# Down projection of a hybrid decoder layer: loads in program order, reloads spread over two loops, two more staging buffers

## The chip, the cores and the metric

The kernel runs on one core of a Trainium2 chip. The metric is the device time of one execution in microseconds, and a smaller one is better. The profile shows the core's engines: PE (TensorE, matmuls; PEld its weight loads), DVE (VectorE), ACT (ScalarE), POOL (GpSimd) and SP (SyncE). In this kernel every DMA is issued from SP, in the order in which SP's instructions stand, and SP waits at an instruction whose semaphores have not come yet.

## The reference, cut to what matters

One decoder layer for 512 tokens and a width of 1024, in float32: two attention mixers, a gated convolutional MLP and a gated embedding. The change is in the MLP's last product (the down projection) and in what is loaded beside it:

```
h  = rmsnorm(x, mlp_pre_norm)
u  = causal_dwconv(h @ w_up)                    # 1024 -> 2 * 2816
ff = (gelu(u_gate) * u_val) @ w_down            # 2816 -> 1024, the down projection
x  = x + rmsnorm(ff, mlp_post_norm)
e  = p @ w_ple
x  = x + sigmoid(rmsnorm(x, ple_norm) @ w_ple_gate) * e
```

## The kernel before, in words

Every float32 product is done as three matmuls: an operand is split into a high part (ACT, L72) and a low part (DVE, L73), and high x high, high x low and low x high are added in PSUM (`mm3`).

**Up projection.** A loop over 22 pairs of 128 columns. PE writes `pu`; ACT and DVE do the convolution and the gelu (L816 to L824). After every second pair, `ff_sums` (L786 to L799) makes from the product `X` of one *chunk* c (0 to 10, 256 hidden units each) the sums that the down projection needs, splits them, keeps the first four in SBUF (`FF[c]`, in the tiles with the tags xh/xl for chunks 0 to 3, kT/qT for 4 to 7, fA/fB for 8 to 10) and writes the others to DRAM: `d1[c]` (512 KB, from `f2h` and `X`) and `d2[c]` (256 KB). The last chunk is chunk 10. `X` and `f2h` live in a pool `qp` that closes when the up projection ends.

**Down projection.** It is a fast product in the manner of Strassen and Winograd, so that seven products do the work of eight. It has three loops over the 11 chunks:

- Loop 1 (L874 to L890): two loads of `w_down` into `raw` tiles per chunk, here called **r1(c)** (L877, 512 KB) and **r2(c)** (L878, 256 KB). DVE forms differences of them (L882 needs r1; L883 and L884 need r2 too) in `T13`/`T2`; ACT and DVE split them; PE does 24 matmuls per chunk, for the products M1, M5, M7 and M6. M1 needs r1 alone; M5 and M7 share one split of 128x1024 that needs r2 as well.
- Loop 2 (L922 to L934): one load per chunk, **raw(c)** (L924, 512 KB), and the reloaded `d1[c]`, **p1(c)** (L915, 512 KB). PE does 12 matmuls per chunk (M1 goes on, and M3).
- Loop 3 (L947 to L952): the product M4, six matmuls per chunk, from the reloaded `d2[c]`, **p2(c)** (L945, 256 KB), and the differences `T4[c]` that loop 2 made.

p1(0..3) goes into the tile with the tag xh, p1(4..7) into xl, and p1(8..10) into xh again: p1(8) can be loaded only once PE has done with p1(0..3). After the loops come the norms (`post_norm`, L725 to L735), transposes (`to_hT`) and the products `pg` and `pe` of the embedding. The norms need the residual `xn` (four reloads of 512 KB, L894) and two gain vectors (L656, 512 KB each).

**What sets the order.** The program is written as a sequence, and a scheduler puts each engine's instructions in an order of its own before the kernel is built; on the chip each engine then keeps that order. Loads into `raw` tiles take a ring of three buffers: a load waits until DVE and ACT have read the buffer's last contents. `hi` and `lo` tiles have rings of four. A pool that is opened where a closed one lay waits for the last readers of what lay there.

Of the kernel before, what the change touches and what calls it, by code (L numbers as in the profile page):

```python
# [8 lines left out]
F32 = mybir.dt.float32  # L9
F32R = mybir.dt.float32r  # L10
# [5 lines left out]
P = 128  # L16
S = 512
NB = 4
# [19 lines left out]
def hybrid_kernel(ctx, tc, T):  # L38
    nc = tc.nc
    act, dve, pool = nc.scalar, nc.vector, nc.gpsimd  # L40
    order = mybir.DependencyInfo(mybir.DependencyClass.NoSync, mybir.DependencyReason.DATA)
# [21 lines left out]
    def opened(**kw):  # L63
        cm = tc.tile_pool(reuse_waits="tile", **kw)
        p = cm.__enter__()
        return p, lambda: cm.__exit__(None, None, None)

    def f32(ap):
        return ap.bitcast(F32)

    def split(hi, lo, src):
        act.activation(hi, src, AF.Copy)  # L72
        dve.tensor_tensor(lo, src, f32(hi), ALU.subtract)  # L73

    def mm3(out, lh, ll, rh, rl, start, stop):
        pe.matmul(out, lh, rh, start=start, stop=False)
        pe.matmul(out, lh, rl, start=False, stop=False)
        pe.matmul(out, ll, rh, start=False, stop=stop)

    def hot(f, *args):  # L80
        with tc.high_priority(HOT):
            return f(*args)
# [23 lines left out]
    xp, close_xp = opened(name="xp", bufs=1, side="left")  # L106
# [14 lines left out]
    W = {"rings": RA, "raw": 0, "hi": 0, "lo": 0}  # L121

    def wtile(kind, dt):
        ring = W["rings"][kind]
        n = W[kind] % sum(c for _, c in ring)
        W[kind] += 1
        for p, c in ring:
            if n < c:
                return p.tile([P, 1024], dt, name="w" + kind, tag="w" + kind, bufs=c)
            n -= c  # L130
# [31 lines left out]
    xh = xp.tile([P, 8, S], F32R, name="xh", tag="xh")  # L162
    xl = xp.tile([P, 8, S], F32R, name="xl", tag="xl")
# [487 lines left out]
    mxl = xp.tile([P, 8, S], F32R, name="mxl", tag="xl")  # L651
    p3 = [accT, accT, scT, scT, scT, ptT, ptT, pvT]

    def loadgain(src):
        t = res["bcp"].tile([P, D], F32, name="gain", tag="gain", bufs=2)
        nc.sync.dma_start(t, src.partition_broadcast(P))  # L656
        return t

    for m in range(8):
# [13 lines left out]
    for f in (close_ca, close_wk, close_gap, close_sp, close_cqp, close_kvp, close_yp):  # L673
# [4 lines left out]
             raw=0, hi=0, lo=0)  # L678
    ck, close_ck = opened(name="ck", bufs=1, side="right")
    fp, close_fp = opened(name="fp", bufs=1, side="right")  # L680

    res = {}

    def open_res():
        b, close_b = opened(name="bcp", bufs=1, side="right")
        x, close_x = opened(name="xnp", bufs=1, side="right")
        res.update(bcp=b, xn=x.tile([P, NB, D], F32, name="xn"), close=(close_x, close_b))

    def close_res():
        for f in res["close"]:  # L690
            f()
# [12 lines left out]
    def banks(n, name):  # L704
        return [bank(n, name) for _ in range(2)]
# [14 lines left out]
    def post_norm(n, ps, gp, gn):  # L720
        xn = res["xn"]
        t = ck.tile([P, D], F32, name="t", tag="t", bufs=3)
        s1, s2, r1, r2, v = (small(f"q{i}", 2 if i == 0 else 1) for i in range(5))
        for h in range(2):
            act.activation(t[:, h * S:(h + 1) * S], ps[h], AF.Square, accum_out=s1[:, h:h + 1])  # L725
        dve.tensor_scalar(v, s1[:, 0:1], 1.0 / D, EPS, ALU.mult, ALU.add)
        dve.scalar_tensor_tensor(v, s1[:, 1:2], 1.0 / D, v, ALU.mult, ALU.add)  # L727
        pool.tensor_tensor(r1, v, mhalf[:, :1], ALU.pow)  # L728
        for h in range(2):
            w = slice(h * S, (h + 1) * S)  # L730
            dve.scalar_tensor_tensor(t[:, w], ps[h], r1, gp[:, w], ALU.mult, ALU.mult)
        dve.tensor_tensor(xn[:, n, :], t, xn[:, n, :], ALU.add)
        act.activation(t, xn[:, n, :], AF.Square, accum_out=s2)
        rsqrt(r2, s2, 1.0 / D, 1)
        dve.scalar_tensor_tensor(t, xn[:, n, :], r2, gn, ALU.mult, ALU.mult)  # L735
        return t
# [17 lines left out]
    for n in range(NB):  # L754
        nc.sync.dma_start(res["xn"][:, n, :], T["x"][n * P:(n + 1) * P, :])
    xd = [dp.tile([P, D], F32, name=f"xd{n}", tag=f"xd{n}") for n in range(NB)]
    g_post, g_next = loadgain(T["attn_post"]), loadgain(T["mlp_pre"])
    ts = {}
    for blocks in ((0, 1), (2,), (3,)):
# [11 lines left out]
    NC = NPAIR // 2  # L771
# [3 lines left out]
    d1 = [dp.tile([P, 2, 2, 256], F32, name=f"d1_{c}", tag=f"d1_{c}") for c in range(NC)]  # L775
    d2 = [dp.tile([P, 2, 256], F32, name=f"d2_{c}", tag=f"d2_{c}") for c in range(NC)]
# [80 lines left out]


    close_qp()
    open_res()  # L860
    xn = res["xn"]
    vp, close_vp = opened(name="vp", bufs=1, side="right")
    T2t = [hp.tile([P, 8, S], F32, name=f"T2{i}", tag=f"hT{i}") for i in range(2)]
    T2 = [T2t[c // 8][:, c % 8] for c in range(NC)]
    T13 = [T2t[1][:, 4 + 2 * i:6 + 2 * i].rearrange("p a t -> p (a t)") for i in range(2)]
    B1, B2 = slice(0, S), slice(S, 2 * S)
# [3 lines left out]
    def mms(ps, lhs, rhs, start, stop):  # L870
        for b in range(2):
            t = slice(b * P, (b + 1) * P)
            mm3(ps[b], lhs[0][:, t], lhs[1][:, t], *rhs, start, stop)

    for c in range(NC):
        r1, r2 = wtile("raw", F32), wtile("raw", F32)
        nc.sync.dma_start(r1, T["wd"][2 * c])  # L877
        nc.sync.dma_start(r2[:, :S], T["wd"][2 * c + 1][:, B2])  # L878
        t13 = T13[c % 2]
        h1, l1, h2, l2 = (wtile(k, F32R) for k in ("hi", "lo", "hi", "lo"))  # L880
        split(h1[:, B1], l1[:, B1], r1[:, B1])
        dve.tensor_tensor(t13[:, B1], r1[:, B2], r1[:, B1], ALU.subtract)  # L882
        dve.tensor_tensor(t13[:, B2], r2[:, :S], r1[:, B2], ALU.subtract)  # L883
        dve.tensor_tensor(T2[c], r2[:, :S], t13[:, B1], ALU.subtract)  # L884
        split(h2, l2, t13)
        split(h1[:, B2], l1[:, B2], T2[c])
        rhs = {"M1": (h1[:, B1], l1[:, B1]), "M5": (h2[:, B1], l2[:, B1]),
               "M7": (h2[:, B2], l2[:, B2]), "M6": (h1[:, B2], l1[:, B2])}
        for m, s in zip(order4, (0, 1, 3, 2)):
            mms(M[m], [t[:, s] for t in FF[c]], rhs[m], c == 0, c == NC - 1)  # L890

    g_post, g_next = loadgain(T["mlp_post"]), loadgain(T["ple_norm"])
    for n in range(NB):
        nc.sync.dma_start(xn[:, n, :], xd[n])  # L894
    T4k = qkp.tile([P, 8, S], F32, name="T4k", tag="kT")
    T4q = qkp.tile([P, 8, S], F32, name="T4q", tag="qT")
    T4 = [T4k[:, c] for c in range(8)] + [T4q[:, 0], T4q[:, 1], vp.tile([P, S], F32, name="T4v")]
    U, V12, C22 = ([T4q[:, 2 + 2 * i + b] for b in range(2)] for i in range(3))

    def drain():  # L900
# [6 lines left out]
            dve.tensor_tensor(C22[b], M["M5"][b], U[b], ALU.add)  # L907

    hot(drain)
    p1 = []  # L910
    for c in range(NC):
        if c % 4 == 0:
            t = xp.tile([P, 4, 2, 2, 256], F32R, name="p1", tag="xl" if c == 4 else "xh")
        p1.append(t[:, c % 4])
        nc.sync.dma_start(f32(p1[c]), d1[c])  # L915
    M3 = banks(3, "M3")

    def m3(c, rhs):
        mms(M3, [p1[c][:, i, 1] for i in range(2)], rhs, c == 0, c == NC - 1)

    late = None
    for c in range(NC):  # L922
        raw = wtile("raw", F32)
        nc.sync.dma_start(raw, T["wd"][2 * c + 1])  # L924
        h, l = wtile("hi", F32R), wtile("lo", F32R)
        split(h, l, raw)
        dve.tensor_tensor(T4[c], raw[:, B1], T2[c], ALU.subtract)
        for b in range(2):
            t = slice(b * P, (b + 1) * P)
            lh, ll = p1[c][:, 0, 0, t], p1[c][:, 1, 0, t]  # L930
            for x, y in ((lh, h), (lh, l), (ll, h)):
                pe.matmul(M["M1"][b], x, y[:, B1], start=False, stop=c == NC - 1 and x is ll, skip_group_check=True)
        if late:
            m3(*late)  # L934
        late = (c, (h[:, B2], l[:, B2]))
# [3 lines left out]
    for n in range(2):  # L939
        dve.tensor_tensor(V12[n], M3[n], V12[n], ALU.add)  # L940
        ts[n] = post_norm(n, (M["M1"][n], V12[n]), g_post, g_next)
    p2t = [fp.tile([P, 6, 2, 256], F32R, name="p2", tag=t) for t in ("fA", "fB")]
    p2 = [p2t[c // 6][:, c % 6] for c in range(NC)]
    for c in range(NC):
        nc.sync.dma_start(f32(p2[c]), d2[c])  # L945
    M4 = banks(2, "M4")
    for c in range(NC):  # L947
        if c % 2 == 0:
            h, l = wtile("hi", F32R), wtile("lo", F32R)
        w = slice(c % 2 * S, (c % 2 + 1) * S)  # L950
        split(h[:, w], l[:, w], T4[c])
        mms(M4, [p2[c][:, i] for i in range(2)], (h[:, w], l[:, w]), c == 0, c == NC - 1)  # L952
# [59 lines left out]
    raw = wtile("raw", F32)  # L1012
    nc.sync.dma_start(raw, T["pT"].rearrange("p a b -> p (a b)"))
    split(ph.rearrange("p a b -> p (a b)"), pl.rearrange("p a b -> p (a b)"), raw)
    for k in range(2):
        raw = wtile("raw", F32)
# [12 lines left out]
    for n in (2, 3):  # L1029
        for half in range(2):  # L1030
# [4 lines left out]
            gate_mms(g, (n,), (half,))  # L1035
            finish(n, half, g[n, half])

    close_vp()
    close_res()
    for f in (close_fp, close_ck, close_rawb, close_qkp, close_rawp, close_psp,  # L1040
              close_hp, close_wb, close_wa, close_xp, close_cpool, close_dp):
        f()
# [89 lines left out]
```

## Time and profile before

| | |
|---|---|
| median of 3 runs (lowest to highest) | 756.83 us (754.61 to 758.09) |
| the profiled execution: its time, its span | 756.0 us, 754.2 us |
| PE busy | 730.6 us (97%) |
| DVE, ACT busy | 533.3 us (71%), 362.8 us (48%) |
| DMA moved | 99.90 MB, mean 132 GB/s |
| chain that ended last | PE 77%, DVE 11%, DMA 9% |

The span runs from the first to the last instruction; the profiled execution's time is 1.8 us longer. On the time line, the up projection ends at 564.8 us, loop 1 runs to 640.1 us, loops 2 and 3 to 687.2 us, and the rest of the kernel takes the last 67 us. A row of the timeline begins with its start and its length in us; the bracket at its end is the idle time before it and what ended it. "Landing" is the time from the issue of a DMA on SP until its data are there.

### The profile page before, as it was taken

The page shows a single profiled execution, that of the slowest core. Times are in us where ns is not written, and L with a number is a line of the kernel's source. Part 1 is how long each engine was busy: PE and PEld are TensorE (multiplying, and loading weights), DVE is VectorE, ACT ScalarE, POOL GpSimd, SP SyncE. Part 2 cuts the span into 40 slices and gives each one's busy share as a digit, 9 for nine tenths or more (in the row PEclk, how much of TensorE's full clock was granted, in tenths as well). Part 3 has the DMA queues.
Part 4 walks back from the last instruction along what each step waited for, and adds up shares of the span by engine and source line. Part 5 has one row for each costly group of instructions (what it writes and reads, how often), then busy time and mean ns, then how long its engine had stood idle before and what let it go on. Part 6 is the DMA issues. An engine that isn't in the chain of part 4 may idle for free.

```text
span 754.2 us, 9531 instructions
## 1 busy us (share of the span) xinstructions
PE 730.6 (97%) x3496; PEld 606.4 (80%) x3496; DVE 533.3 (71%) x939; ACT 362.8 (48%) x634; POOL 49.8 (7%) x46
## 2 busy tenths in 40 slices
PE   9999999999999989999999999999999869998997
PEld 8988878778888868898888888888887658876886
DVE  6568787986785493848776777676759657789832
ACT  5843677755453243627435444544435234266631
POOL 0104023000000070200000000000000000001000
PEclk9999999999999999999999999999999979999999
DMA  8612221121122455324343434334314874943311
GB/s 301 243 42 63 60 84 43 57 79 63 56 84 59 164 189 174 129 95 140 126 152 127 152 128 139 130 105 143 116 66 157 319 294 151 378 151 112 113 56 56
DMA packets 36239, 99.90 MB, mean 132 GB/s; under 512 B 4481, under 2 KB 8577, under 8 KB 36193
## 3 DMA queue, kind: packets, MB, share of 16 engines
q1 hardware_dynamic: 36192, 99.30, 38.8%
q8 instruction: 27, 0.44, 0.3%
q14 instruction: 20, 0.16, 0.1%
HBM read 85.98 MB, written 12.85 MB: 131 GB/s over the span
## 4 chain that ended last, share of the span: by engine, by line
PE 77%; DVE 11%; DMA 9%; issue 2%; ACT 1%; SPq 0%; ACTq 0%; DVEq 0%
PE pu L56 29%; PE psg L56 11%; DMA wraw<-in_wd 7%; PE yo L56 6%; PE pg L56 6%; DVE wlo L73 3%; PE puh L56 3%; PE M L56 3%; PE psA L56 3%; PE psba L56 3%; PE psC L56 2%; PE psB L56 2%; PE pe L56 1%; PE scm L56 1%; PE pb L56 1%
## 5 line engine op out<-in xcount | busy, mean ns | idle before, releaser
L56 PE MATMUL pu<-hT,whi 128*128 128x512 f32 x640 | 197.0, 389 | 0.0
L72 ACT ACTIVATE whi<-wraw 128x1024 fp32r<-128x1024 f32 (+4 forms) x109 | 106.5, 979 | 162.9 <-PE pu L56 75.2
L73 DVE TENSOR_TENSOR wlo<-wraw,whi 128x1024 fp32r<-128x1024 f32 (+2 forms) x103 | 119.4, 1161 | 65.7 <-ACT whi L72 62.0
L56 PEld LDWEIGHTS pu<-hT,whi 128*128 128x128 f32 x640 | 120.1, 188 | 25.0
L56 PE MATMUL pu<-hT,wlo 128*128 128x512 f32 x320 | 124.5, 389 | 0.0
L56 PEld LDWEIGHTS pu<-hT,wlo 128*128 128x128 f32 x320 | 60.1, 188 | 12.3
L56 PE MATMUL psg<-xh,whi 128*128 128x512 f32 x128 | 51.7, 404 | 1.0 <-DVE ga L422 0.9
L56 PE MATMUL psg<-xl,whi 128*128 128x512 f32 x128 | 51.3, 401 | 0.0
L56 PE MATMUL psg<-xh,wlo 128*128 128x512 f32 x128 | 51.2, 400 | 0.0
L56 PE MATMUL M<-whi,p 128*128 128x512 f32 x132 | 41.4, 393 | 1.0 <-ACT whi L72 1.0
L72 ACT ACTIVATE whi<-T 128x1024 fp32r<-128x1024 f32 (+1 forms) x22 | 17.8, 838 | 38.3 <-DVE T L883 38.2
L816 ACT ACTIVATE cv<-pu,pp 128x512 f32<-128x512 f32 x40 | 30.6, 765 | 9.1 <-PE pu L56 9.1
L817 DVE SCALAR_TENSOR_TENSOR cv<-pu,pp,cv 128x511 f32<-128x511 f32 x40 | 29.8, 745 | 4.3 <-ACT cv L816 4.3
L818 DVE SCALAR_TENSOR_TENSOR cv<-pu,pp,cv 128x510 f32<-128x510 f32 x40 | 29.9, 747 | 1.1
L819 ACT ACTIVATE cv<-cv 128x512 f32<-128x512 f32 x22 | 13.9, 632 | 34.2 <-DVE cv L818 34.2
L56 PEld LDWEIGHTS M<-whi,p 128*128 128x128 f32 x132 | 24.7, 188 | 6.8 <-ACT whi L72 1.4
L728 POOL TENSOR_TENSOR q<-q,mhalf 128x1 f32<-128x1 f32 x8 | 5.3, 674 | 375.5 <-DVE q L727 369.7
L56 PEld LDWEIGHTS psg<-xh,whi 128*128 128x128 f32 x128 | 24.5, 191 | 6.5 <-DVE ga L422 1.1
L56 PEld LDWEIGHTS psg<-xl,whi 128*128 128x128 f32 x128 | 24.4, 191 | 5.0 <-issue 0.2
L56 PEld LDWEIGHTS psg<-xh,wlo 128*128 128x128 f32 x128 | 24.4, 190 | 4.9
L56 PE MATMUL M<-wlo,p 128*128 128x512 f32 x66 | 26.0, 394 | 0.1
L670 POOL TENSOR_TENSOR gx<-gx,ga 128x512 f32<-128x512 f32 x8 | 14.8, 1869 | 133.3 <-DVE gx L669 133.3
(304 smaller groups left out, 1585.9 us busy)
## 6 DMA issues: line engine op xcount, KB each, us to landing
wraw<-in_wup SPq DMA_DIRECT2D x44, 512.0 KB, 3.5
wraw<-in_wd SPq DMA_DIRECT2D x22, 512.0 KB, 4.3
wraw<-in_wg SPq DMA_DIRECT2D x16, 512.0 KB, 3.3
p<-d SPq DMA_DIRECT2D x11, 512.0 KB, 9.6
wraw<-in_wo SPq DMA_DIRECT2D x8, 512.0 KB, 4.1
wraw<-in_wpg SPq DMA_DIRECT2D x8, 512.0 KB, 3.4
d<-f2h SPq DMA_DIRECT2D x11, 256.0 KB, 3.1
d<-X SPq DMA_DIRECT2D x11, 256.0 KB, 2.0
```

The source lines that it names most:

```text
L56: pe.chain(out, nc.tensor.matmul(out, *a, **k))
L72: act.activation(hi, src, AF.Copy)
L73: dve.tensor_tensor(lo, src, f32(hi), ALU.subtract)
L670: pool.tensor_tensor(ta, ta, ga[:, m, :], ALU.add)
L728: pool.tensor_tensor(r1, v, mhalf[:, :1], ALU.pow)
L816: act.activation(c, u, AF.Identity, scale=w2, bias=cb)
L817: dve.scalar_tensor_tensor(c[:, 1:], u[:, :S - 1], w1, c[:, 1:], ALU.mult, ALU.add)
L818: dve.scalar_tensor_tensor(c[:, 2:], u[:, :S - 2], w0, c[:, 2:], ALU.mult, ALU.add)
L819: act.activation(cs[0], cs[0], AF.Gelu_apprx_tanh)
```

## The change

All loads of the down projection go through a helper `load`, which ties each load to the one before it, so that SP issues them in the order of the program. The reloads p1(0) to p1(7) stand in loop 1, behind the chunks 5 to 10; p1(8) to p1(10), the gains, the residual and p2 stand in loop 2. For loop 1 the ring of raw buffers has two more (pool `rx`, five in all), which lie where the closed pool `qp` lay; the pools of the gains and the residual are opened after loop 1, where they were opened before it.

```diff
-    def loadgain(src):
+    def loadgain(src, go=nc.sync.dma_start):
         t = res["bcp"].tile([P, D], F32, name="gain", tag="gain", bufs=2)
-        nc.sync.dma_start(t, src.partition_broadcast(P))
+        go(t, src.partition_broadcast(P))
         return t
...
     close_qp()
-    open_res()
-    xn = res["xn"]
     vp, close_vp = opened(name="vp", bufs=1, side="right")
+    T4v = vp.tile([P, S], F32, name="T4v")
+    rx, close_rx = opened(name="rx", bufs=1, side="right")
+    R2 = W["rings"]["raw"]
+    W["rings"]["raw"] = R2 + [(rx, 2)]
+    loads = []
+
+    def load(dst, src):
+
+        i = nc.sync.dma_start(dst, src).ins
+        if loads:
+            tc.add_manual_dep(i, loads[-1], order, reason="load order")
+        loads.append(i.name)
+
+    p1 = []
+
+    def load_p1(c):
+        if c % 4 == 0:
+            load_p1.t = xp.tile([P, 4, 2, 2, 256], F32R, name="p1", tag="xl" if c == 4 else "xh")
+        p1.append(load_p1.t[:, c % 4])
+        load(f32(p1[c]), d1[c])
...
     for c in range(NC):
         r1, r2 = wtile("raw", F32), wtile("raw", F32)
-        nc.sync.dma_start(r1, T["wd"][2 * c])
-        nc.sync.dma_start(r2[:, :S], T["wd"][2 * c + 1][:, B2])
+        load(r1, T["wd"][2 * c])
+        load(r2[:, :S], T["wd"][2 * c + 1][:, B2])
...
-    g_post, g_next = loadgain(T["mlp_post"]), loadgain(T["ple_norm"])
-    for n in range(NB):
-        nc.sync.dma_start(xn[:, n, :], xd[n])
+        for i in {5: (0,), 6: (1,), 7: (2,), 8: (3,), 9: (4, 5), 10: (6, 7)}.get(c, ()):
+            load_p1(i)
+
+    close_rx()
+    W["rings"]["raw"] = R2
+    open_res()
+    xn = res["xn"]
...
-    p1 = []
-    for c in range(NC):
-        if c % 4 == 0:
-            t = xp.tile([P, 4, 2, 2, 256], F32R, name="p1", tag="xl" if c == 4 else "xh")
-        p1.append(t[:, c % 4])
-        nc.sync.dma_start(f32(p1[c]), d1[c])
...
     for c in range(NC):
         raw = wtile("raw", F32)
-        nc.sync.dma_start(raw, T["wd"][2 * c + 1])
+        load(raw, T["wd"][2 * c + 1])
+        if c in (4, 5, 6):
+            load_p1(c + 4)
+        if c in (3, 4, 5, 6):
+            load(xn[:, c - 3, :], xd[c - 3])
+        if c == 2:
+            g_post, g_next = loadgain(T["mlp_post"], load), loadgain(T["ple_norm"], load)
+        if c == 7:
+            p2t = [fp.tile([P, 6, 2, 256], F32R, name="p2", tag=t) for t in ("fA", "fB")]
+            p2 = [p2t[c // 6][:, c % 6] for c in range(NC)]
+        if c >= 7:
+            for i in range(3 * (c - 7), min(3 * (c - 6), NC)):
+                load(f32(p2[i]), d2[i])
...
-    p2t = [fp.tile([P, 6, 2, 256], F32R, name="p2", tag=t) for t in ("fA", "fB")]
-    p2 = [p2t[c // 6][:, c % 6] for c in range(NC)]
-    for c in range(NC):
-        nc.sync.dma_start(f32(p2[c]), d2[c])
```

**SP at the end of the up projection, before.** `wraw` with in_wd is a load of w_down (128x1024 is r1, 128x512 is r2; here r1(0), r2(0), r1(1), then r2(1) and so on); d1_9, d2_9, d1_10 and d2_10 are the writes of the last two chunks to DRAM.

```order
L877 DMA wraw_5012<-in_wd 128x1024
L878 DMA wraw_5013<-in_wd 128x512
L877 DMA wraw_5053<-in_wd 128x1024
L798 DMA d1_9_3118<-f2h_4828 128x512
L799 DMA d2_9_3129<-f2h_4828 128x256
L798 DMA d1_9_3118<-X_4749 128x512
L799 DMA d2_9_3129<-X_4749 128x256
L878 DMA wraw_5054<-in_wd 128x512
L877 DMA wraw_5094<-in_wd 128x1024
```

The first chunk's two loads and one of the second stand ahead of the writes of chunk 9; those of chunk 10 come ten rows further down. The same place with the change:

```order
L869 DMA wraw_5009<-in_wd 128x1024
L798 DMA d1_9_3118<-f2h_4828 128x512
L799 DMA d2_9_3129<-f2h_4828 128x256
L798 DMA d1_9_3118<-X_4749 128x512
L799 DMA d2_9_3129<-X_4749 128x256
L798 DMA d1_10_3119<-f2h_4984 128x512
L799 DMA d2_10_3130<-f2h_4984 128x256
L798 DMA d1_10_3119<-X_4905 128x512
L799 DMA d2_10_3130<-X_4905 128x256
L869 DMA wraw_5010<-in_wd 128x512
L869 DMA wraw_5050<-in_wd 128x1024
L869 DMA wraw_5051<-in_wd 128x512
```

r1(0) alone is still ahead; r2(0) (`wraw_5010`) and every load behind it now stand behind the writes of chunk 10.

**DVE at the same place, with the change.** L901 to L903 are what L882 to L884 were (the differences of a chunk of w_down); L817 to L796 finish chunk 10 of the up projection.

```order
L901 TENSOR_TENSOR T_5000<-wraw 128x512
L817 SCALAR_TENSOR_TENSOR cv<-pu,pp,cv 128x511
L818 SCALAR_TENSOR_TENSOR cv<-pu,pp,cv 128x510
L824 TENSOR_TENSOR X<-cv 128x2x256
L788 TENSOR_TENSOR X<-X 128x256
L790 TENSOR_TENSOR X<-X 128x256
L791 TENSOR_TENSOR X<-X 128x256
L73 TENSOR_TENSOR fffB<-X,fffA 128x1024
L796 TENSOR_TENSOR X<-X,f2h 128x768
L902 TENSOR_TENSOR T_5000<-wraw 128x512
L903 TENSOR_TENSOR T_4999<-wraw,T_5000 128x512
```

Before, the rows of chunk 10 stood between those of the down projection's chunks 0 to 3; now they stand in one piece, between the first difference of chunk 0 and its second.

**SP in loop 2, with the change.** From raw(4) (`wraw_5567`) to raw(7) (`wraw_5631`); the bracket names the engines that a load waits for (DMAHW is an earlier DMA).

```order
L869 DMA wraw_5567<-in_wd 128x1024 [waits DMAHW6_49,DMAHW4_49,DVE_49]
L869 DMA p1_5569<-d1_8_3117 128x1024 [waits PE_49]
L869 DMA xn_5477<-xd1_2797 128x1024
L869 DMA wraw_5589<-in_wd 128x1024 [waits DMAHW7_49,DVE_49]
L869 DMA p1_5569<-d1_9_3118 128x1024 [waits DMAHW0_49]
L869 DMA xn_5477<-xd2_2798 128x1024 [waits DMAHW1_49]
L869 DMA wraw_5610<-in_wd 128x1024 [waits DMAHW2_49,DVE_49]
L869 DMA p1_5569<-d1_10_3119 128x1024 [waits DMAHW3_49]
L869 DMA xn_5477<-xd3_2799 128x1024 [waits DMAHW4_49]
L869 DMA wraw_5631<-in_wd 128x1024 [waits DMAHW5_49,DVE_49]
```

And before, where p1(8) to p1(10) stood behind raw(7), and three loads of w_down behind them:

```order
L924 DMA wraw_5608<-in_wd 128x1024
L945 DMA p2_5752<-d2_9_3129 128x512
L945 DMA p2_5752<-d2_10_3130 128x512
L924 DMA wraw_5627<-in_wd 128x1024
L915 DMA p1_5494<-d1_8_3117 128x1024
L915 DMA p1_5494<-d1_9_3118 128x1024
L915 DMA p1_5494<-d1_10_3119 128x1024
L924 DMA wraw_5646<-in_wd 128x1024
L924 DMA wraw_5665<-in_wd 128x1024
L924 DMA wraw_5684<-in_wd 128x1024
```

p1(8), which waits for PE, stood behind raw(7) (`wraw_5627`) and now stands ahead of raw(5) (`wraw_5589`); the reloads of the residual, which were issued in loop 1, now stand between the loads of w_down.

## Rows read from the trace of the kernel before

**Rows 1.** The page: PE's granted clock and the DMA engines' share in 40 slices.

```profile
PEclk9999999999999999999999999999999979999999
DMA  8612221121122455324343434334314874943311
```

**Rows 2.** Timeline of PE, the waits of the down projection and the stages' first matmuls.

```profile
567.24 1.89 PE L56 MATMUL M<-whi,ffxh 128*128 128x512 f32 x7 [0.89 <-ACT whi L72]
...
606.61 3.78 PE L56 MATMUL M<-whi,ffkT 128*128 128x512 f32 x8 [5.40 <-ACT whi L72]
...
617.39 2.35 PE L56 MATMUL M<-whi,ffkT 128*128 128x512 f32 x6 [2.82 <-ACT whi L72]
...
640.11 0.62 PE L56 MATMUL M<-whi,p 128*128 128x512 f32 x2
...
663.06 1.19 PE L56 MATMUL M<-whi,p 128*128 128x512 f32 x4 [1.03 <-ACT whi L72]
...
687.19 1.03 PE L60 MATMUL ptr<-ident,t 128*128 128x128 f32 x8
```

**Rows 3.** Timeline of DVE: the difference that the second wait hung on.

```profile
604.69 0.69 DVE L883 TENSOR_TENSOR T<-wraw 128x512 f32<-128x512 f32 x1 [7.85 <-DMA wraw<-in_wd]
```

**Rows 4.** Timeline of SP, the queue ahead of that load, DMAs as issued.

```profile
588.36 0.40 SPq L878 DMA_DIRECT2D wraw<-in_wd  x1
...
591.08 2.31 SPq L894 DMA_DIRECT2D xn<-xd  x4
593.80 0.33 SPq L878 DMA_DIRECT2D wraw<-in_wd  x1
```

**Rows 5.** DMA issues, loads issued at 593.80, 566.12 and 545.39: KB, us to landing.

```profile
wraw<-in_wd SPq DMA_DIRECT2D x1, 256.0 KB, 10.9
...
wraw<-in_wd SPq DMA_DIRECT2D x1, 256.0 KB, 2.8
...
wraw<-in_wd SPq DMA_DIRECT2D x1, 512.0 KB, 3.4
```

**Rows 6.** Windows: stretch, its length, each engine's busy us, PEclk, DMA share, GB/s.

```profile
606.60:610.20 3.60, 3.59 (x9) 2.82 (x10) 2.47 (x4) 0.99 (x2) 0.00 (x0) 0.50 1.03 409
610.20:611.40 1.20, 1.20 (x5) 0.97 (x4) 0.00 (x0) 0.00 (x0) 0.00 (x0) 0.56 1.03 413
617.40:620.40 3.00, 3.00 (x9) 2.33 (x9) 2.70 (x5) 0.99 (x2) 0.00 (x0) 0.61 0.73 257
...
642.00:650.00 8.00, 8.00 (x37) 6.64 (x36) 7.18 (x11) 2.12 (x2) 0.00 (x0) 1.00 0.99 358
...
655.00:661.00 6.00, 6.00 (x29) 4.95 (x28) 2.86 (x3) 1.06 (x1) 0.00 (x0) 1.00 1.02 410
```

**Rows 7.** Timelines of ACT and DVE: one of each step that finishes an up chunk.

```profile
565.03 0.78 ACT L816 ACTIVATE cv<-pu,pp 128x512 f32<-128x512 f32 x1 [2.37 <-PE pu L56]
579.79 1.06 ACT L72 ACTIVATE fffA<-X 128x1024 fp32r<-128x1024 f32 x1
...
560.40 0.75 DVE L817 SCALAR_TENSOR_TENSOR cv<-pu,pp,cv 128x511 f32<-128x511 f32 x1 [2.72 <-ACT cv L816]
577.26 0.41 DVE L788 TENSOR_TENSOR X<-X 128x256 f32<-128x256 f32 x1
583.02 1.21 DVE L73 TENSOR_TENSOR fffB<-X,fffA 128x1024 fp32r<-128x1024 f32 x1
586.50 0.94 DVE L796 TENSOR_TENSOR X<-X,f2h 128x768 fp32r<-128x768 f32 x1
```

**Rows 8.** Groups of PE instructions from 640 to 663: count, busy us, mean ns.

```profile
L56 PE MATMUL M<-whi,p 128*128 128x512 f32 x64 | 19.9, 389 | 0.0
L56 PE MATMUL M<-wlo,p 128*128 128x512 f32 x32 | 12.4, 389 | 0.0
```

**Rows 9.** Timeline of DVE: the last difference of loop 2, and the first transposed block.

```profile
665.92 0.68 DVE L927 TENSOR_TENSOR T4v<-wraw,T 128x512 f32<-128x512 f32 x1
691.65 1.28 DVE L748 TENSOR_TENSOR h3T<-ptr,h3T 128x512 fp32r<-128x512 f32 x2
```

More of the change, by code (lines that the diff above doesn't have):

```diff
@@ L890, in hybrid_kernel @@
             mms(M[m], [t[:, s] for t in FF[c]], rhs[m], c == 0, c == NC - 1)
-    g_post, g_next = loadgain(T["mlp_post"]), loadgain(T["ple_norm"])
-    for n in range(NB):
-        nc.sync.dma_start(xn[:, n, :], xd[n])
+        for i in {5: (0,), 6: (1,), 7: (2,), 8: (3,), 9: (4, 5), 10: (6, 7)}.get(c, ()):
[4 more added lines that the diff above has]
+    xn = res["xn"]
     T4k = qkp.tile([P, 8, S], F32, name="T4k", tag="kT")
     T4q = qkp.tile([P, 8, S], F32, name="T4q", tag="qT")
-    T4 = [T4k[:, c] for c in range(8)] + [T4q[:, 0], T4q[:, 1], vp.tile([P, S], F32, name="T4v")]
+    T4 = [T4k[:, c] for c in range(8)] + [T4q[:, 0], T4q[:, 1], T4v]
     U, V12, C22 = ([T4q[:, 2 + 2 * i + b] for b in range(2)] for i in range(3))
@@ L1036, in hybrid_kernel @@
             finish(n, half, g[n, half])
+    close_res()
     close_vp()
-    close_res()
     for f in (close_fp, close_ck, close_rawb, close_qkp, close_rawp, close_psp,
```

## Prediction, made before the changed kernel was run

> **What bounds the kernel now.** I read the page's slices first [rows 1]: PE's clock and the DMA share are even everywhere but in slices 32 to 36 of 40 (585 to 680 us), where the DMA share is 0.8, 0.7, 0.4, 0.9 and 0.4 and the clock of one slice falls to 0.7. That is the down projection. The timeline of PE shows there where the time goes [rows 2]: four pauses, 0.89, 5.40, 2.82 and 1.03 us, each ended by an ACT split of freshly loaded weights. Elsewhere PE runs without a gap, so PE bounds the kernel but for these 10.1 us, and what each leaves behind: after the second and third, PE ran at 0.50, 0.56 and 0.61 of its clock, that is partly at 1.2 GHz where it had 2.4 before the pause [rows 6].
>
> The view of DVE says why the longest came: it sat 7.85 us until r2 of a chunk landed [rows 3]. That load was issued at 593.80 and took 10.9 us [rows 4, 5], against 2.8 for one of the same 256 KB on a quiet queue [rows 5]. Right ahead of it stood the four reloads of the residual, 2 MB [rows 4], which only the norms behind loop 2 read. So reloads that nothing needs yet go in front of the weights that PE needs at once. The change aims at this burst. The place to ask is therefore which load PE waits for in the new order of SP.
>
> **The change part by part.**
>
> *Burst removed from loop 1.* Residual and gains leave it, and the p1 come one or two per chunk behind a chunk's own weights. Gone are the pauses of 5.40 and 2.82 us [rows 2] and their slow clock: 3.60 us at 0.50 cost 1.8, 1.20 at 0.56 cost 0.5, 3.00 at 0.61 cost 1.2 [rows 6], and I take 0.5 more behind the last by the pattern of the first. Sum: 5.40 + 2.82 + 1.8 + 0.5 + 1.2 + 0.5 = **-12.2**. Nothing takes their place inside loop 1: a chunk brings 0.77 MB and at most two p1 (1.05 MB) in the 5.5 us or so that its 24 matmuls take, some 330 GB/s against the 410 that the queue has moved [rows 6], and five buffers hold two and a half chunks. p1(0) waits on SP until PE has done chunk 3, but by then chunks 4 and 5 are loaded. If that cover is thinner than I think, up to 2 us come back.
>
> *A new hole at the start of loop 1.* The two new buffers lie where `qp` lay, and on SP r2(0) now stands behind the four writes of chunk 10, which wait for ACT and DVE to finish that chunk. Before, r2(0) and r1(1) stood ahead even of the writes of chunk 9, and PE's seventh matmul of loop 1 began at 567.24 [rows 2]. Now PE has only M1's six matmuls of chunk 0. The chain for the seventh, from the last `pu` result: ACT L816 begins at 565.03 and takes 0.78; DVE L817, L818 and L824, three of 0.75 or less; L788, L790, L791, 0.41 each; the split on ACT 1.06 and on DVE 1.21; L796 0.94 [rows 7]: 565.03 + 0.78 + 2.25 + 1.23 + 1.06 + 1.21 + 0.94 = 572.5. From the end of such an L796 (586.50 + 0.94) over two writes to the next load (588.36) took 0.92 [rows 4, 7], so r2(0) is issued at 573.4 and lands 2.8 later [rows 5], at 576.2. From landing to PE it took 604.69 to 606.61, 1.92 [rows 2, 3]: PE goes on at 578.1, **+10.9** against 567.24. The pause of some 12 us is longer than the 5.40 that cost 2.3 of clock, so **+2.3** more. Bounds: neighbouring rows overlap by up to 0.4 in all, and the load may take the 3.4 of a 512 KB one; 12.8 to 13.8 for both. Loop 1 then ends at about +1.0, at 641.
>
> *Blocked loads in loop 2.* p1(8) goes into the tile of p1(0..3) and so waits for PE to finish chunk 3 of loop 2; the loads keep their order, so xn1, raw(5) and all behind queue up after it. Before, the three p1 of this tile stood behind raw(7), with three loads still to come, and the pause at 663.06 was 1.03 [rows 2]. With S for the start of loop 2 (640.11 before): 96 matmuls took 663.06 - 1.03 - 640.11 = 21.9 us [rows 2, 8], 0.228 each. Four chunks are 48 matmuls, so p1(8) is issued at S + 10.9. A 512 KB load alone lands in 3.4 [rows 5], and each further 512 KB takes 1.28 at 410 GB/s [rows 6]; raw(5) is the third, landing at S + 16.9, and its split is 1.06 by a row of the same shape [rows 7]: PE starts chunk 5 at S + 18.0, where chunk 4 ended at S + 13.7. From there the queue is one unbroken stream of 16.5 x 512 KB up to raw(10) (xn2, xn3, p1(9), p1(10) and nine p2 stand between the weights): S + 10.9 + 3.4 + 15.5 x 1.28 = S + 34.1. Of this the nine p2 (4.5 x 512 KB) are the small kind, and where these were queued the rate was 358 GB/s, 1.46 for 512 KB (from 642 to 650) [rows 6]; with 4.5 x 0.18 = 0.8 more, raw(10) lands at S + 34.9 and is split at S + 36.0. Then chunk 10 and M4, 78 matmuls. Loops 2 and 3 took 687.19 - 640.11 = 47.1 for 198 matmuls, less 1.03 and some 0.4 taken for slow clock behind it 0.231 each, so M4 ends at S + 36.0 + 18.0 = S + 54.0: **+6.9** against 47.1. The lower bound is raw(5)'s wait alone, 4.3 and some 1.2 of clock less the 1.4 that goes: +4.1. The upper one has the whole stream at that 358: 15.5 x 0.18 = 2.8 on top of 6.1, +8.9.
>
> The Trainium skill ("DMA: Bandwidth & Descriptors", section "Where 436 GB/s comes from") says that for transfers between HBM and SBUF the HBM side binds at about 358 GB/s. The 8 us with p2 in the queue agree with it, but the 6 us behind them do not, at 410 on this one core [rows 6], and the measurement decides; by the page the whole stream would go at that rate, and the sum would be 2.0 longer.
>
> *Residual, gains and p2 later.* Nothing waits for them: the gains land by S + 5 and the residual by S + 25, while the norms that read them come after chunk 10; the last p2 lands some 1.5 behind raw(10), and M4 comes to it ten chunks later.
>
> *The tail.* DVE is nearly full behind loop 2. From the last difference (665.92) to the first transposed block (691.65) it had 25.7 us of work [rows 9]; that block was 4.5 behind M4's end. With raw(10) landing at S + 34.9 and the same list, it comes at S + 60.6, 6.6 behind M4's end; some of the list waited for PE or POOL and shrinks. I take **+0.5** (0 to 2.1).
>
> Sum against the profiled execution's own time: 756.0 - 12.2 + 10.9 + 2.3 + 6.9 + 0.5 = **764.4**. That execution is 0.8 under the median of 756.83, inside the runs' spread. What a measurement can tell from no change is about 0.5%, 3.8 us.
>
> **The rivals.**
>
> *Faster.* The burst is the whole story, and the two new buffers fill the loop. "Perfetto Trace Analysis" in the Trainium skill (section "Identifying the Most-Contended Engine") says that the same gap coming again can mean too little SBUF for the next tile, and that would speak for five buffers. As a mechanism here: r2(0) is in SBUF when the up projection ends, and raw(5) was issued before p1(8) blocks. Then 756.0 - 12.2 - 1.4 = 742.4; with the hole of loop 2 alone, 756.0 - 12.2 + 7.4 = 751.2. For it: the two big pauses did hang on that burst. Against it: the order of SP leaves no way round the writes of chunk 10.
>
> *No change.* The hole at the start comes, but loop 2 runs as before: 756.0 + 1.0 - 1.4 = 755.6. That needs raw(5) to land some 4 us earlier than I find, hence SP to pass p1(8) by S + 7, when PE is in the middle of chunk 2. Against it: p1(8) is tied to PE.
>
> *Slower still.* The stream of loop 2 goes at 358 GB/s from raw(5) on, not only where p2 stand in it, and DVE's list ends the full 2.1 later: 756.0 + 1.0 + 8.9 + 2.1 = 768.0. For it: no row shows weights, p1, residual and p2 mixed as they will be. Against it: the stretch at 410 carried weights and p1 side by side, by the order of SP.
>
> *That the change does nothing* can be left out: SP's order has changed.
>
> **How the numbers follow.** Forecast 0.58 (its own range 760 to 767.5), slower still 0.18, no change 0.12, faster 0.12. The range of 755 to 770 takes in the no-change case, the forecast and most of the slower one, and leaves out the faster one and the far end: 0.17. Faster than -0.5% (under 753) 0.12; within 0.5% 0.13, the no-change case and a sliver of the forecast; slower (over 760.6) 0.75.
>
> **What would show it.** A pause of 10 to 12 us on PE right after six M matmuls at 566, ended by a split whose r2 was issued behind the writes from `X`; no pause above 1 us from there to the end of loop 1, which ends at 641 give or take 2; in loop 2 a pause of 4 to 5 us before chunk 5, with p1(8) issued when chunk 3 ends, and pauses below 1 us behind it; M4's end near 695. I am wrong if r2(0) is issued before 570, if raw(5) lands before PE has done chunk 4, or if loop 1 has a new pause that I took as covered.

## The result: slower by 1.35%, about as forecast

| | before | after |
|---|---|---|
| median of the compared runs, us | 757.46 (754.61 to 758.93, 4 runs) | 767.14 (766.63 to 768.39, 4 runs) |
| profiled execution, us (its span) | 756.0 (754.2) | 768.39 (766.6) |
| first matmul of loop 1 to first of loop 2 | 75.28 | 75.80 |
| first of loop 2 to first transpose | 47.08 | 55.93 |
| first transpose to the end of the span | 67.0 | 68.8 |

The ratio is 1.0135, with a 95% interval of 1.0101 to 1.0168. The forecast was 764.4 (755 to 770), with 0.75 on slower. The two spans differ by 12.4 us, the medians by 9.7, because the profiled execution of after is the slowest of its four and that of before lies 1.5 under its median. The 12.4 fall into four parts, from first matmuls: 1.24 ahead of loop 1, which begins at 566.07 where it began at 564.83 (the second kernel below differs from after in loop 2 alone and begins it at 563.78, so this is scatter), 0.52 in loop 1, 8.85 in loops 2 and 3, 1.8 in the tail.

The page's slices of after, PE's granted clock and the DMA share, show the move at once, beside those of before [rows 1]. From slice 31 on the DMA share is now even, 0.7, 0.5, 0.6, 0.6, 0.8, 0.6, where it went 0.4, 0.8, 0.7, 0.4, 0.9, 0.4. The low clock has left slice 33, the middle of loop 1, for slices 30 and 31, its start, and 35, loop 2.

```profile
PEclk9999999999999999999999999999987999899999
DMA  8711221212112633515433434343117566863311
```

The timeline of PE (start, duration, line, operation, count, idle time ahead and what ended it), in answer to [rows 2]:

```profile
566.07 0.39 PE L56 MATMUL M<-whi,ffxh 128*128 128x512 f32 x1
...
580.29 2.07 PE L56 MATMUL M<-whi,ffxh 128*128 128x512 f32 x4 [12.70 <-ACT whi L72]
...
641.87 0.63 PE L56 MATMUL M<-whi,p 128*128 128x512 f32 x2
...
661.40 2.08 PE L56 MATMUL M<-whi,p 128*128 128x512 f32 x4 [5.72 <-ACT whi L72]
...
697.80 1.09 PE L60 MATMUL ptr<-ident,t 128*128 128x128 f32 x8 [0.29 <-DVE t L735]
699.80 0.50 PE L56 MATMUL pg<-whi,h3T 128*128 128x512 f32 x1 [0.91 <-ACT h3T L747]
703.19 1.00 PE L60 MATMUL ptr<-ident,t 128*128 128x128 f32 x4 [2.19 <-DVE h3T L748]
```

The four pauses of the three loops, 10.1 us, have become two of 18.4: one at the seventh matmul of loop 1, one before chunk 5 of loop 2. Between 580 and 641 PE does not stop. The queue of SP, in answer to [rows 4], has the cause of both:

```profile
573.88 0.42 SPq L799 DMA_DIRECT2D d<-X  x1
574.40 16.25 SPq L869 DMA_DIRECT2D wraw<-in_wd  x11
...
642.28 0.37 SPq L869 DMA_DIRECT2D wraw<-in_wd  x1
652.99 0.33 SPq L869 DMA_DIRECT2D p<-d  x1
653.36 0.43 SPq L869 DMA_DIRECT2D xn<-xd  x1
653.89 0.38 SPq L869 DMA_DIRECT2D wraw<-in_wd  x1
```

r2(0) goes out at 574.40, right behind the writes from `X` of chunk 10. In loop 2, SP issues nothing between raw(4) at 642.28 and p1(8) at 652.99, 10.7 us later; that p1 waits for PE, and raw(5) stands two loads behind it, although its buffer was free: the last reader of raw(2), which had lain there, was DVE's split at 642.06, 1.21 long.

The timeline of DVE has the finish of chunk 10 (L796), the landing of r2(0) and the first transposed block (compare [rows 3, 9]):

```profile
572.53 0.95 DVE L796 TENSOR_TENSOR X<-X,f2h 128x768 fp32r<-128x768 f32 x1
578.46 0.69 DVE L902 TENSOR_TENSOR T<-wraw 128x512 f32<-128x512 f32 x1 [4.98 <-DMA wraw<-in_wd]
...
677.83 0.69 DVE L955 TENSOR_TENSOR T4v<-wraw,T 128x512 f32<-128x512 f32 x1 [0.91 <-DMA wraw<-in_wd]
...
702.45 1.27 DVE L748 TENSOR_TENSOR h3T<-ptr,h3T 128x512 fp32r<-128x512 f32 x2
```

Windows of after (length, busy time of PE, PEld, DVE, ACT, POOL, then granted clock, DMA share, GB/s), in answer to [rows 6]:

```profile
578.00:582.00 4.00, 1.71 (x4) 1.42 (x5) 3.53 (x5) 2.10 (x3) 0.00 (x0) 0.50 0.99 338
...
660.00:666.00 6.00, 4.60 (x11) 3.69 (x12) 3.40 (x4) 2.11 (x2) 0.00 (x0) 0.52 1.02 416
666.00:672.00 6.00, 5.95 (x25) 4.33 (x25) 3.05 (x4) 1.78 (x2) 0.00 (x0) 1.00 1.04 396
672.00:678.00 6.00, 5.88 (x23) 3.67 (x22) 3.31 (x4) 1.50 (x3) 0.00 (x0) 1.00 1.04 397
```

After each pause PE comes back at 0.50 of its clock, 1.2 GHz, for some 4 us. And the stream of loop 2, with weights, p1, residual and p2 in it, ran at 396 to 416 GB/s from 660 on; in its first 6 us, from 654, it had moved 330.

### The profile page after: what moved, and what is told of

The parts are those of the page before. It is cut to its first block, busy times and chain, and to the rows that moved or that the text cites. A ratio compares the mean times of both kernels' runs of the same rounds, so it can differ in the third digit from the quotient of the medians.

```text
span 766.6 us, 9527 instructions
## 1 busy us (share of the span) xinstructions
PE 733.7 (96%) x3496; PEld 607.4 (79%) x3496; DVE 535.2 (70%) x939; ACT 362.5 (47%) x634; POOL 51.5 (7%) x46
## 4 chain that ended last, share of the span: by engine, by line
PE 83%; DVE 9%; DMA 4%; issue 1%; ACT 1%; SPq 1%; POOL 0%; DVEq 0%; ACTq 0%; POOLq 0%
PE pu L56 28%; PE psg L56 11%; PE M L56 9%; PE yo L56 6%; PE pg L56 6%; PE puh L56 3%; PE psA L56 3%; PE psba L56 2%; DMA wraw<-in_wd 2%; PE psC L56 2%; DVE wlo L73 2%; PE psB L56 2%; PE scm L56 2%; PE pe L56 1%; PE pb L56 1%
## 5 line engine op out<-in xcount | busy, mean ns | idle before, releaser
L56 PE MATMUL M<-whi,p 128*128 128x512 f32 x132 | 44.0, 410 | 5.7 <-ACT whi L72 5.7
L817 DVE SCALAR_TENSOR_TENSOR cv<-pu,pp,cv 128x511 f32<-128x511 f32 x40 | 29.8, 744 | 4.7 <-ACT cv L816 4.7
L72 ACT ACTIVATE whi<-T 128x1024 fp32r<-128x1024 f32 (+1 forms) x22 | 18.0, 839 | 22.2 <-DVE T L902 11.8
L56 PE MATMUL pg<-whi,h3T 128*128 128x512 f32 (+1 forms) x72 | 23.3, 389 | 0.9 <-ACT h3T L747 0.9
```

What stands on the lines that cost most here:

```text
L56: pe.chain(out, nc.tensor.matmul(out, *a, **k))
L817: dve.scalar_tensor_tensor(c[:, 1:], u[:, :S - 1], w1, c[:, 1:], ALU.mult, ALU.add)
```

## The experiments

The theory: three things act, each by itself: the burst's removal (-12), the two buffers' hole (+13) and p1(8) ahead of raw(5) (+7). The rivals were that the buffers are what fills loop 1, that loop 2 is bound by the bytes moved into it, and that one of order and spreading is the whole cure. The runs of before beside the first four kernels gave 757.72, beside the last three 755.69; each ratio is to its own. Where the edits are parts of one another, differences of ratios are turned into us with 757.

**One: after without the two buffers.**

```diff
-    W["rings"]["raw"] = R2 + [(rx, 2)]
```

> The changed kernel with loop 1 on the three raw buffers that it had before (the pool rx is opened but not used); order and spreading of the loads as changed. My theory: the hole of 12.7 us at the start of loop 1 is there only because two of the first five buffers lie on the closed pool, so it goes (a pause of about 1 us as before, and no slow clock), three buffers suffice for loop 1 once no burst stands ahead, and the pause of 5.7 us in loop 2 stays: 767.1 - 11.8 - 2.3 = 753 us (751 to 755). Rival: the two buffers are what keeps loop 1 free of pauses; then pauses of 2 us and more come back in loop 1 and the time is 757 to 762.

Measured: 755.24 (10 runs), ratio 0.9975 (0.9961 to 0.9989). From PE's timeline:

```profile
568.13 1.88 PE L56 MATMUL M<-whi,ffxh 128*128 128x512 f32 x7 [0.89 <-ACT whi L72]
...
628.85 0.98 PE L56 MATMUL M<-whi,p 128*128 128x512 f32 x2 [0.20 <-ACT T4q L923]
...
650.15 2.07 PE L56 MATMUL M<-whi,p 128*128 128x512 f32 x4 [5.62 <-ACT whi L72]
```

Loop 1 runs on three buffers with no pause but the first 0.89. From its first matmul (565.72) to loop 2 it takes 63.13, against 75.28 in before: 12.15 less, where the prediction had 12.2 for the burst. So the buffers cost 0.0160 of the time, 12.1 us, and fill nothing in loop 1. The pause of loop 2 is still there, as it should be; from 628.85 to the first transpose at 686.57 it is 57.7 us, against 47.08, and that eats most of what loop 1 gained, so that the median is 2 us above the 753 expected.

**Two: after with p1(8..10) behind raw(7), where before had them.**

```diff
-        if c in (4, 5, 6):
-            load_p1(c + 4)
...
+        if c == 7:
+            for i in (8, 9, 10):
+                load_p1(i)
```

> The changed kernel with the reloads p1(8) to p1(10) behind raw(7) and no longer behind raw(4), raw(5) and raw(6). My theory: SP's wait for PE at p1(8) is what holds raw(5) up; the pause before chunk 5 goes with its slow clock, loops 2 and 3 take 47 to 48 us from the first p1 matmul to the first transpose where they took 55.6, and the time is 758 to 760 us. Rival: loop 2 is bound by the bytes that were moved into it; then raw(10) lands at most 2 us earlier than with the change, the wait only moves to a later chunk, and the time is 765 to 767.

Measured: 759.93 (7 runs), ratio 1.0036 (1.0014 to 1.0059). PE's timeline:

```profile
578.52 3.78 PE L56 MATMUL M<-whi,ffxh 128*128 128x512 f32 x8 [13.22 <-ACT whi L72]
...
663.44 1.20 PE L56 MATMUL M<-whi,p 128*128 128x512 f32 x4 [1.18 <-ACT whi L72]
```

The hole of loop 1 stays, the pause of loop 2 shrinks from 5.72 to 1.18, and loops 2 and 3 take 48.56 in place of 55.93, with the same bytes moved. The place of three loads is worth 0.0099, 7.5 us; the prediction had 6.9. The rival of the bytes wanted 765 us or more.

**Three: both edits.**

> Both edits together: three raw buffers in loop 1, and p1(8) to p1(10) behind raw(7). My theory: both holes are gone and the gain from the burst that was spread is left: 745 us (743 to 748), with no pause of PE above 1 us between 566 and 690. The rivals (two buffers needed, or loop 2 bound by its bytes): 752 us and more.

Measured: 750.08 (4 runs), ratio 0.9900 (0.9876 to 0.9925), faster than before, but 5 us above the 745 expected and outside its range. A pause is left in loop 2, and the queue of SP shows why:

```profile
655.04 2.07 PE L56 MATMUL M<-whi,p 128*128 128x512 f32 x4 [2.79 <-ACT whi L72]
```

```profile
642.36 3.02 SPq L868 DMA_DIRECT2D p<-d  x6
645.48 0.86 SPq L868 DMA_DIRECT2D wraw<-in_wd  x1
646.39 3.17 SPq L868 DMA_DIRECT2D p<-d  x3
650.58 0.33 SPq L868 DMA_DIRECT2D wraw<-in_wd  x1
```

raw(8) stands behind six p (three p1, three p2) and raw(9) behind three more p2, which nothing reads before loop 3.

Nor need the two edits simply add. Without the buffers p1(8)'s place is worth 0.0075, 5.7 us (one against three); with p1(8) out of the way the buffers cost 0.0136, 10.3 us (two against three). By the intervals these are not clearly less than 7.5 and 12.1, but the traces go the same way: where the hole of loop 1 is gone, loops 2 and 3 take longer, 57.72 in one against 55.93 in after, 52.82 here against 48.56 in two.

**Four: before, with its loads merely tied to the order of the program.** Gains, residual and p1(0..7) then stand between the two loops' weights in one piece.

```diff
+        if loads:
+            tc.add_manual_dep(i, loads[-1], order, reason="load order")
...
-        nc.sync.dma_start(r1, T["wd"][2 * c])
+        load(r1, T["wd"][2 * c])
...
```

> The kernel before with nothing but the order: every load of the down projection is tied to the one before it, three raw buffers, and the gains, the residual and p1(0) to p1(7) stay in one piece between loop 1 and loop 2 (p1(8) to p1(10) stand behind raw(7), since in front of raw(0) they would wait for ever). My theory: the order alone takes the burst out of loop 1 (its two pauses of 5.4 and 2.8 us go, 12.2 us with the slow clock) but puts 7.3 MB ahead of raw(0), 18 us at 410 GB/s from the issue of r2(10) some 13 us before the loop's end: a pause of 8 to 9 us at the start of loop 2 and 2.3 of slow clock, 755 to 758 us in all. Rival: the order is the whole cure and the spreading adds nothing: 745 to 748.

Measured: 757.25 (10 runs), ratio 1.0002 (0.9984 to 1.0019).

```profile
639.97 2.07 PE L56 MATMUL M<-whi,p 128*128 128x512 f32 x4 [12.33 <-ACT whi L72]
```

```profile
615.80 2.19 SPq L866 DMA_DIRECT2D xn<-xd  x4
618.10 9.51 SPq L866 DMA_DIRECT2D p<-d  x8
628.56 18.73 SPq L866 DMA_DIRECT2D wraw<-in_wd  x7
```

The burst has only moved: loop 1 has no pause but its 0.89, and all of it comes at the start of loop 2. It is 12.33 us long where 8 to 9 were expected: raw(0) went out only at 628.56, behind fourteen reloads (the two gains are right ahead of these rows), and was split 10.3 us later. Order without spreading is worth nothing.

**Five: as three, and all p2 behind raw(10).**

```diff
-        if c >= 7:
-            for i in range(3 * (c - 7), min(3 * (c - 6), NC)):
+        if c == NC - 1:
+            for i in range(NC):
                 load(f32(p2[i]), d2[i])
```

> The changed kernel without its two extra buffers and with p1(8..10) behind raw(7), as in e3, and now with all eleven p2 behind raw(10) as well (no p2 between the weights of loop 2). Theory (the pause of 2.79 us that e3 had left came from raw(9), which was issued at 650.58 behind six reloads of p1 and p2): that pause is gone or under 0.8 us, loops 2 and 3 take 50.5 us or less against 52.8 in e3, and since no second weight split stands ahead of the last norm's product on DVE any more, the first block after M4 is transposed as before (pause at h3T about 1.5 us, tail 67.0 against 68.5). Time 746 to 747 us (745 to 748.5). Rival (raw(9) was late because a ring of three buffers is too short, whatever is queued): the pause stays, 749.5 to 750.5, and only the tail gives something.

Measured: 746.25 (743.33 to 748.96, 4 runs), ratio 0.9855 (0.9825 to 0.9885): the fastest version here, better than both kernels. The pause of 2.79 is gone, and loops 2 and 3 take 48.8 (628.60 to 677.37), 4.0 less than in the third. For the whole kernel the two intervals overlap a little, so its lead over the third is likely, not settled. A smaller pause is left early in loop 2, and this one is for a low part from DVE:

```profile
635.51 0.50 PE L56 MATMUL M<-wlo,p 128*128 128x512 f32 x1 [1.55 <-DVE wlo L73]
```

The first and the third have such pauses too, 1.06 in the one, 0.82 and 0.74 in the other; the other kernels have none. They go with the longer loops 2 and 3 noted above; what delays these splits was not followed up.

The pause ahead of the last transposes is 1.55 again as expected, but the tail is not 67.0: it takes 69.8, and the reason is the clock (last section).

**Six: as five, with the two buffers from chunk 2 on.**

```diff
+        if c == 2:
+            W["rings"]["raw"] = R2 + [(rx, 2)]
```

> As e6, but with the two extra raw buffers in the ring from chunk 2 of loop 1 on (the first two chunks take the three old ones). Theory (the buffers cost time only because the first chunk's r2 was laid into memory that the up projection still used): r2(0) is issued early again, no pause at the seventh matmul of loop 1, and five buffers give nothing there since loop 1 has no pauses without them: the same time as e6 within 1 us. Rival (any use of that memory holds up the loads, or more loads in flight delay others): a pause of over 3 us at chunk 1 or 2 of loop 1, and 750 or more.

Measured: 750.74 (5 runs), ratio 0.9929 (0.9899 to 0.9959), 0.0074 or 5.6 us worse than the fifth (the medians are 4.5 apart). My theory fell here, and the rival came true but for the chunk. Chunk 0 has no more than its 0.89, but a pause of 3.82 comes at chunk 3. PE's and SP's timelines:

```profile
586.63 0.73 PE L56 MATMUL M<-whi,ffxh 128*128 128x512 f32 x2 [3.82 <-ACT whi L72]
```

```profile
565.43 5.04 SPq L868 DMA_DIRECT2D wraw<-in_wd  x3
...
581.38 0.43 SPq L799 DMA_DIRECT2D d<-X  x1
581.85 6.45 SPq L868 DMA_DIRECT2D wraw<-in_wd  x6
```

The loads of chunk 3 are again issued right behind the last write from `X`. With three buffers, in five, eight weight loads go out in the same stretch, where here there are three, ahead of the first write of chunk 10, which is issued at 584.12:

```profile
566.39 16.43 SPq L868 DMA_DIRECT2D wraw<-in_wd  x8
```

So it is any load into that memory, not the first one alone, that is late until chunk 10 is written; a later start makes the hole smaller (3.82 for 12.70), not free. That the memory is what ties them is read from the order alone; the buffers were not tried in other memory. Loop 1 takes 5.96 more than in the fifth (69.47 for 63.51) and loops 2 and 3 take 3.05 less (45.72 for 48.77, the shortest here, with no pause for DVE), so part of what the pause of loop 1 costs comes back behind it.

**Seven: as five, without the tie to the program's order.**

```diff
-        if loads:
-            tc.add_manual_dep(i, loads[-1], order, reason="load order")
```

> As e6, but the loads are no longer tied to the order of the program, so SP's order is the scheduler's again: the gains and the four residual reloads then stand ahead of the loads of the last chunks of loop 1, as in the kernel before. Theory (it is the place of that burst ahead of the weights that costs): pauses of 3 to 8 us in the second half of loop 1 again, with slow clock behind them, and 753 to 758 us. Rival (spreading the p1 in the program is enough, the fixed order does nothing): the same as e6, 746 to 748.

Measured: 757.47 (10 runs), ratio 1.0004 (0.9984 to 1.0024).

```profile
588.36 3.46 SPq L868 DMA_DIRECT2D p<-d  x6
592.38 1.61 SPq L868 DMA_DIRECT2D wraw<-in_wd  x2
...
598.71 4.79 SPq L868 DMA_DIRECT2D xn<-xd  x4
604.53 34.93 SPq L868 DMA_DIRECT2D wraw<-in_wd  x12
```

```profile
605.10 3.58 PE L56 MATMUL M<-whi,ffkT 128*128 128x512 f32 x8 [5.38 <-ACT whi L72]
615.92 2.93 PE L56 MATMUL M<-whi,ffkT 128*128 128x512 f32 x6 [3.49 <-ACT whi L72]
```

Bursts are back in the middle of loop 1, with two pauses, 5.38 and 3.49, as in before [rows 2]. The expectation named gains and residual; they stand ahead of the second pause alone, whose load was issued at 604.53. The load that the first pause hung on was issued at 592.38, behind six p1 in one piece, and landed 10.8 us later. So without the tie the scheduler undoes the spreading too. The tie is worth 0.0149, 11.3 us, once the places behind it are right.

## Why the prediction was right, step by step

*Burst, -12.2.* Right: 12.15 with three buffers, and nothing took its place inside loop 1. But it was two bursts: the load behind the pause of 5.40 was the one behind the residual, that behind the pause of 2.82 was issued at 606.03, behind seven p1. Both had to be spread.

*Hole at the start of loop 1, +10.9 and +2.3.* Right in mechanism. The chain from the last `pu` result to L796 ends at 572.53 + 0.95 = 573.5 where 572.5 was forecast, of which 1.2 is the late start of this execution. The seventh matmul came at 580.29, 13.05 later than in before, 11.8 without that start. The rest of the miss is one row: r2(0) landed 4.0 us after its issue, not 2.8. Three more weight loads went out within 1.9 us behind it; that these slowed it is likely, not shown. Clock included, loop 1 took 0.52 more than before, +1.0 was forecast.

*p1(8) ahead of raw(5), +6.9.* Right in mechanism, short in size: +8.85, the upper bound of its range. Against S, the first matmul of loop 2, p1(8) went out at S + 11.1 (10.9 forecast), and PE resumed at S + 19.5 (18.0) after a pause of 5.72 (4.3): from the issue of p1(8) to the landing of raw(5) 7.2 us passed, not 6.0, 0.9 of them until SP had issued raw(5) and 6.3 until it landed, in the 6 us at 330 GB/s where 410 had been taken. From there the weights came at the pace of the stream, and PE took each at once: the timeline of ACT has one split every 3.3 to 3.9 us, each ended by a DMA, of which these are the first and the last,

```profile
660.29 1.06 ACT L72 ACTIVATE whi<-wraw 128x1024 fp32r<-128x1024 f32 x1 [10.09 <-DMA wraw<-in_wd]
...
677.91 1.06 ACT L72 ACTIVATE whi<-wraw 128x1024 fp32r<-128x1024 f32 x1 [2.25 <-DMA wraw<-in_wd]
```

so raw(10) was there at S + 36.0 (34.9 forecast). PE's timeline has the start of chunk 10 in the row right behind,

```profile
678.70 1.98 PE L56 MATMUL M<-whi,p 128*128 128x512 f32 x7
```

whose first matmul still belongs to the work ahead of it; the next, the first behind raw(10)'s split, begins at 679.03, S + 37.2 (36.0 forecast). The 78 matmuls from there took 18.5 to M4's end at 697.51 (18.0). With the 0.29 that the first transpose waited for the norm these make the 1.9: 1.2 + 0.5 + 0.3, rounded. What made the 78 matmuls 0.5 longer was not followed up.

*The tail, +0.5 of 0 to 2.1.* Mis-sized: 1.8, and by a term that I had not counted. The first transposed block came at S + 60.6, as forecast, but by luck: the last difference was 1.1 late and DVE's list behind it 1.1 shorter (24.62 from 677.83 to 702.45 against 25.73 [rows 9]). The two waits of PE behind the first transpose sum to 3.10 against 2.97 in before: +0.1. The other 1.7 is clock: behind the pause of 2.19 PE had 0.67, 0.50 and 0.81, which over 1, 2 and 2 us is 0.3 + 1.0 + 0.4,

```profile
703.00:704.00 1.00, 0.81 (x5) 0.82 (x6) 0.98 (x5) 0.46 (x1) 0.00 (x1) 0.67 0.82 217
704.00:706.00 2.00, 2.00 (x6) 1.62 (x6) 1.42 (x3) 0.98 (x2) 1.06 (x2) 0.50 0.36 145
706.00:708.00 2.00, 2.00 (x8) 1.59 (x8) 2.00 (x4) 1.17 (x2) 0.00 (x0) 0.81 0.00 0
```

while the clock in before did not fall in the tail.

*The total.* That 764.4 lies so near the median of 767.14 is in part luck. Without the scatter ahead of loop 1 the trace has +11.2 (0.52 + 8.85 + 1.8) where +8.4 was forecast (1.0 + 6.9 + 0.5): loop 1 came out 0.5 better than forecast, loops 2 and 3 1.9 worse and the tail 1.3 worse, and the medians rose by 9.7 only.

*The rivals.* "Faster" failed where it was said to: r2(0) was not in SBUF, and raw(5) was behind p1(8). The rule of the Trainium skill that was weighed for it ("Perfetto Trace Analysis", where it stands in the section "Optimization Strategy": the same gap again and again can mean too little SBUF for the next tile) names a cause that was not the one here: with three buffers loop 1 keeps no pause but the first 0.89. "No change" failed because raw(5) landed at S + 18.3, when PE had done with chunk 4 (S + 13.8). "Slower still" gave 768.0, closer to the median than the forecast, but not by its mechanism: it wanted the stream from raw(5) on at 358 GB/s, and the windows above show 396 to 416 there (raw(10) landed 17.7 us after raw(5), where the forecast had 18.0). That also speaks against the 358 GB/s that the Trainium skill's "DMA: Bandwidth & Descriptors" (section "Where 436 GB/s comes from") lets bind between HBM and SBUF, for a core that works alone; the measurement decides. What held the stretch at 358 in before [rows 6] stays open.

## What to carry to other kernels

A queue that issues in order should have, at each place, only loads whose buffers are already free: one load that waits for PE (p1(8), 5.7 to 7.5 us here) or lies, as the order has it, in memory that the stage before still uses (the extra buffers, 10.3 to 12.1 us) holds up every load behind it, however early that one could go. Here spreading the reloads paid only together with a fixed order, and a fixed order only with the spreading: each alone gave nothing (1.0004 and 1.0002), both with the right places 0.9855. Do not add up such prices as if each stood alone: in the three pairs of traces here, the loops behind took 1.8 to 4.3 us longer where the hole of loop 1 was gone. Price a pause with the clock behind it, and count that price as a chance, not as a constant.

## What the runs showed of the hardware

The clock after a short pause is not settled by the length of the pause. Kernels four and five have the same two waits in the tail, 1.42 and 1.55 us; here are the second wait's end in PE's timeline and the windows behind it, for four and then for five:

```profile
692.67 0.66 PE L60 MATMUL ptr<-ident,t 128*128 128x128 f32 x4 [1.55 <-DVE h3T L748]
```

```profile
694.70:696.70 2.00, 2.00 (x11) 1.65 (x10) 2.00 (x5) 1.06 (x1) 0.00 (x0) 1.00 0.08 31
```

```profile
682.57 1.12 PE L60 MATMUL ptr<-ident,t 128*128 128x128 f32 x4 [1.55 <-DVE h3T L748]
```

```profile
684.40:686.40 2.00, 2.00 (x6) 1.59 (x5) 2.00 (x4) 1.06 (x1) 0.00 (x0) 0.50 0.07 27
```

One went on at 2.4 GHz, the other at 1.2 for some 6 us, and its tail is 2.8 us longer. Of the five kernels with these two waits (to 0.02), before and four went on at 1.00, and five, six and seven fell to 0.50. Five, six and seven ran on another chip than four, but the runs of before spread alike on both (754.41 to 760.20 and 754.57 to 758.75); what decides stays open. The spread between runs of one kernel may be the same thing: of the 36 runs of before beside these experiments, the 11 below 756 us had a mean granted clock of 0.990 to 0.991, the 14 above 758 had 0.984 to 0.988; 0.004 of 754 us is 3 us. That the difference sits in the tail of those runs is not shown, since only one execution of a kernel has a trace.
